# A two-layer encoder on one core: the w_down operands of a seven-product down projection formed beside the up product and kept in DRAM

## The chip, the cores and the metric

The kernel runs on one core of one Trainium2 chip. The metric is the device time of one execution in microseconds (us), the median of the runs. The core has five engines with a queue each: PE (matmul), DVE (VectorE), ACT (ScalarE), POOL (GpSimd) and SP (SyncE), which here issues every transfer. An engine runs its own instructions strictly in their order, and a waiting instruction holds up all those behind it.

## The reference, cut to what matters

Two layers, x of 1024 rows by 1024 columns, all float32. Each layer has four groups of attention heads with an output projection, and then a gated MLP with D_FF = 2816:

```python
h = _rmsnorm(x, norm2_g[l])
u = h @ w_up[l]
...
u = _dwconv3(u, conv_w[l], conv_b[l])
gate, val = split of u into two halves of 2816 columns
x = x + (silu(gate) * val) @ w_down[l]
```

`_dwconv3` is a convolution of width 3 along the rows, one weight per tap and column, and a bias.

## The kernel before, in words

Every product is made in float32 by three matmul passes: an operand is split into a high part (a cast on ACT, L136) and a low part (source minus high part, L132, on DVE or POOL), and PE sums high·high, high·low and low·high. `split` (L128 to L132) does this for all weights.

**The end of the attention** (`tail`). While the last heads finish, PE makes the output projection `od` row block by row block. Each block is added to the residual `xacc`, squared on ACT (L157) for the norm's statistic, scaled to `nx`, transposed by PE (`ntp`, L147) and split into `h2T` (cast L173 on ACT, low part L174 on DVE). `h2T` has two tiles, one for each half of the rows. The order of PE's work here and of the attention is written out by hand in the kernel; the order on the other engines is set by the scheduler that builds the program. `mlp` starts in this stretch: it loads the convolution's weights `cw` (L919, L920) and the first up weights (`load`, L922 to L927).

**The up product** (`mlp`, L913). 44 column blocks of 128 (22 gate blocks, 22 value blocks, taken in pairs). For each, SP loads 512 KB `rawu`, ACT casts it and POOL makes the low part (tile `wu`, three buffers); PE makes 48 matmuls of 128x512 into one of two PSUM buffers `u`; the convolution is one ACT instruction (L939) and two on DVE (L940, L941), which read PSUM. Per pair, ACT makes the Silu (L946) and POOL the product (L948, L952). The first 8 of the 22 gated chunks go to DRAM (`gd`, L949), the other 14 stay in SBUF (`gg`).

**The down product** (`down`, L990). It is a scheme of seven products instead of eight for a 2 by 2 block matrix (table `DOWN`, L978). Each product has 11 steps, each step 12 matmuls of 128x512, so 77 steps and 924 matmuls in each layer. A step has two operands, both made on the spot:

- the gated side: one chunk, or the sum or difference of two chunks (DVE, L1006; 55 of the 77 steps), then cast on ACT and low part on DVE;
- the side of w_down: one or two loads of 256 KB (L1020); where there are two, POOL adds or subtracts them (L1006; 55 steps); then cast on ACT, low part on POOL for odd c and on DVE for even c.

Both lie in one tile `wd` of tag wu, three buffers. Product 0 also reloads the 8 gated chunks from DRAM (`gb`, L1026). At the end of each product DVE adds its sums from PSUM into `xacc` (L1037), 4 or 8 instructions, 48 in each layer.

Of the kernel before, what the change touches and what calls it, by code (L numbers as in the profile page):

```python
# [24 lines left out]
S = 1024  # L25
# [65 lines left out]
class K:  # L91
# [821 lines left out]
    def mlp(self, l, h2T, mp, gd):  # L913
# [8 lines left out]
        def load(jj):  # L922
            raw = self.raw.tile([128, KC, 128], F32, tag="raw", name="rawu")
            nc.sync.dma_start(raw, a["w_up"][l, jj])
            w = mp.tile([128, 2, KC, 128], F32R, tag="wu", name="wu", bufs=3)
            self.split((w[:, 0], w[:, 1]), raw, "act", "pool")
            return w  # L927
# [16 lines left out]
        def gate(j, us):  # L944
# [8 lines left out]
            return t  # L953
# [11 lines left out]
        gp, pm = yield  # L965
        for j in range(1, NFF):
            us = []
            for jj in (j, NFF + j):
                w = load(jj)
                u = pm.tile([128, S], F32, tag="u", name="u", bufs=2)  # L970
                product(u, w, (0, 1))
                us.append(conv(jj, u))
# [17 lines left out]
    def down(self, l, xacc, gs, rx, gp, mp, pm, gd):  # L990

        nc, a = self.nc, self.a
        V, P = nc.vector, nc.gpsimd
        NH = NFF // 2
        todo = [j for c in range(GD // 2) for j in (2 * c, 2 * c + 1)]
        back = {}
        for j in todo[0::2] + todo[1::2]:
            back[j] = gs[j] = gp.tile([128, S], F32, tag=f"b{j}", name="gb")
        order = list(range(GD // 2, NH)) + list(range(GD // 2))

        def operand(w, tag, terms, add, low):
            t = terms[0][0]
            if len(terms) > 1:
                u, sign = terms[1]
                d = mp.tile([128, S], F32, tag="c", name="sum", bufs=3)[:, 0:512] if tag == "ga" else t
                add.tensor_tensor(d, t, u, op=ALU.add if sign > 0 else ALU.subtract)  # L1006
                t = d
            self.split((w[:, 0], w[:, 1]), t, "act", low)
        for n, (As, Bs, Cs) in enumerate(self.DOWN):
# [5 lines left out]
            for i, c in enumerate(order):  # L1015
                raw = (rx if i % 3 == 2 else self.raw).tile([128, 2, 512], F32, tag="raw", name="rawd")
                tb = []
                for q, (k, j, sign) in enumerate(Bs):
                    r0 = (2 * c + k) * 128
                    nc.sync.dma_start(raw[:, q], a["w_down"][l, r0:r0 + 128, j * 512:(j + 1) * 512])  # L1020
                    tb.append((raw[:, q], sign))
                if n == 0 and i >= 1:
                    for _ in range(2):
                        if todo:
                            j = todo.pop(0)
                            nc.sync.dma_start(back[j], gd[j * 128:(j + 1) * 128, :])  # L1026
                w2 = mp.tile([128, 2, 2, 512], F32R, tag="wu", name="wd", bufs=3)
                w, m = w2[:, 0], w2[:, 1]
                operand(w, "ga", [(gs[2 * c + k][:, i * 512:(i + 1) * 512], sign) for i, k, sign in As], V, "dve")
                operand(m, "wd", tb, P, "pool" if c % 2 else "dve")  # L1030
# [112 lines left out]
    def run(self):  # L1143
# [16 lines left out]
        for l in range(self.depth):  # L1160
# [76 lines left out]
            gd = dp.tile([GD * 128, S], F32, tag=f"gd{l}", name=f"gd{l}")  # L1237

# [4 lines left out]
            def mlp():  # L1243
                if "mlp" not in st:
                    ae.close()
                    st["mp"] = me.enter_context(self.pool(f"mp{l}", side=at))
                    h2.append(high.enter_context(self.pool(f"h2b{l}", side=at)).tile([128, 2, KC, 512], F32R, name="h2T1"))
                    st["mlp"] = self.mlp(l, h2, st["mp"], gd)
# [61 lines left out]
            g = st["mlp"].send((ge, pm))  # L1310
            high.close()
            self.down(l, xacc, g, ge, high.enter_context(self.pool(f"Gb{l}", side=at)), st["mp"], pm, gd)
            high.close()
# [35 lines left out]
```

## Time and profile before

| what | us |
|---|---|
| median of three runs | 3204.69 (3200.09 to 3205.86) |
| the profiled execution | 3198.61 |
| its span in the trace | 3196.8 |
| PE busy | 2972.4 (93% of the span) |
| DVE, ACT, POOL busy | 1958.1, 1509.8, 1079.8 |
| mean granted TensorE clock | 0.984 of full |

In the profile's rows a start is given in us from the start of the span; "x12" is the number of instructions that a row joins; what stands in brackets is the idle time of the engine just before, and the instruction that ended it. PEclk is the share of its full clock that TensorE was granted. The first layer's MLP lies at about 845 to 1612 us, the second's at 2433 to 3190 us.

### The profile page before, as it was taken

To read this page: it belongs to the slowest core of one execution; us is meant where nothing else is said; L and a number is where in the kernel's file an instruction comes from. 1 tells how busy PE (TensorE), PEld (TensorE's weight loads), DVE (VectorE), ACT (ScalarE), POOL (GpSimd) and SP (SyncE) were. 2 spreads that over 40 slices of the span, in tenths; PEclk is the share of its full clock that TensorE was granted. 3 is DMA by queue.
4 is the path that set the end of the run, shared out by engine and by line. 5 is a ranking of instruction groups with operands and counts; after the bars stand their busy time and mean duration, and the time that the engine had idled before them with its cause. 6 is when DMAs were issued, how large, how long until landed. Compare 5 with 4: busy or idle time off the path is not lost. (4 is left out here: it accounts for less than half of the span.)

```text
span 3196.8 us, 44677 instructions
## 1 busy us (share of the span) xinstructions
PE 2972.4 (93%) x16536; PEld 2550.3 (80%) x16536; DVE 1958.1 (61%) x3352; ACT 1509.8 (47%) x2873; POOL 1079.8 (34%) x916
## 2 busy tenths in 40 slices
PE   7988899899899999998989899998998999999988
PEld 5978888788788888876779788887886888888767
DVE  6778877777622222277966798777776222223787
ACT  5557765766522222233354677657655222222333
POOL 1265310320133333346522663104102333333464
PEclk9999999999999999999999899999999999999999
DMA  4332241331311111144433322314302211111444
GB/s 144 114 101 67 62 128 39 84 78 45 48 57 69 59 51 49 47 161 158 168 123 111 96 67 70 121 43 93 83 24 41 73 73 54 52 47 69 166 157 161
DMA packets 313162, 275.96 MB, mean 86 GB/s; under 512 B 201200, under 2 KB 246640, under 8 KB 312944
## 3 DMA queue, kind: packets, MB, share of 16 engines
q1 hardware_dynamic: 312944, 273.11, 27.8%
q8 instruction: 130, 2.13, 0.3%
q14 instruction: 88, 0.72, 0.1%
HBM read 212.23 MB, written 50.33 MB: 82 GB/s over the span
## 5 line engine op out<-in xcount | busy, mean ns | idle before, releaser
L143 PE MATMUL u<-h2T,wu 128*128 128x512 f32 x4224 | 963.3, 390 | 0.0
L143 PEld LDWEIGHTS u<-h2T,wu 128*128 128x128 f32 x4224 | 792.7, 188 | 168.9
L940 DVE SCALAR_TENSOR_TENSOR c<-u,cw,c 128x1023 f32<-128x1023 f32 x88 | 112.9, 1282 | 721.2 <-ACT c L939 717.6
L143 PE MATMUL pj<-w,hT 128*128 128x256 f32 (+2 forms) x3072 | 490.0, 313 | 21.3 <-ACT w L136 8.4
L143 PEld LDWEIGHTS pj<-w,hT 128*128 128x128 f32 x3072 | 440.1, 194 | 48.3 <-ACT w L136 9.9
L132 POOL TENSOR_TENSOR wu<-rawu,wu 128x1024 fp32r<-128x1024 f32 x88 | 214.2, 2435 | 626.3 <-ACT wu L136 626.3
L939 ACT ACTIVATE c<-u,cw 128x1024 f32<-128x1024 f32 x88 | 106.2, 1207 | 634.5 <-PE u L143 634.5
L489 ACT CAST PT<-pt 128x512 fp32r<-128x512 f32 x448 | 261.4, 583 | 179.5 <-PE pt L147 170.5
L490 DVE TENSOR_TENSOR PT<-pt,PT 128x512 fp32r<-128x512 f32 x448 | 304.7, 684 | 44.6 <-ACT PT L489 42.1
L147 PE MATMUL pt<-cst,P 128*128 128x128 f32 x1792 | 276.7, 277 | 54.3 <-DVE PT L490 47.9
L143 PE MATMUL d<-wd 128*128 128x512 f32 x1056 | 256.2, 401 | 30.1 <-POOL wd L132 16.7
L143 PEld LDWEIGHTS ot<-PT,v 128*128 128x128 f32 x1664 | 255.4, 192 | 32.0
L147 PEld LDWEIGHTS pt<-cst,P 128*128 128x128 f32 x1792 | 208.1, 142 | 87.8 <-issue 33.8
L143 PE MATMUL ot<-PT,v 128*128 128x256 f32 x1664 | 271.0, 286 | 0.0
L143 PEld LDWEIGHTS d<-wd 128*128 128x128 f32 x1056 | 200.6, 193 | 84.2 <-POOL wd L132 26.1
L143 PE MATMUL S<-k,q 96*128 96x512 f32 (+2 forms) x512 | 209.3, 435 | 17.9 <-DVE nmb L655 16.0
L1006 POOL TENSOR_TENSOR rawd<-rawd 128x512 f32<-128x512 f32 x110 | 164.5, 1496 | 149.5 <-DMA rawd<-in_w_down_dram 145.8
L143 PE MATMUL od<-wo,mT 128*128 128x512 f32 x768 | 202.0, 402 | 0.9 <-DVE mT L1067 0.7
L143 PE MATMUL du<-wd 128*128 128x512 f32 x792 | 186.8, 393 | 12.6 <-POOL wd L132 8.8
L143 PEld LDWEIGHTS du<-wd 128*128 128x128 f32 x792 | 146.9, 188 | 51.6 <-POOL wd L132 13.1
L136 ACT CAST wd<-rawd 128x512 fp32r<-128x512 f32 x154 | 95.4, 619 | 179.6 <-POOL rawd L1006 171.9
L655 DVE CUSTOM_DVE_ANT_0 P<-S,toep 128x1024 f32<-128x1024 f32 x128 | 155.4, 1217 | 25.6 <-PE pt L147 21.7
(212 smaller groups left out, 4565.8 us busy)
## 6 DMA issues: line engine op xcount, KB each, us to landing
rawd<-in_w_down_dram SPq DMA_DIRECT2D x264, 256.0 KB, 3.0
rawu<-in_w_up_dram SPq DMA_DIRECT2D x88, 512.0 KB, 3.2
rawi<-in_w_in_dram SPq DMA_DIRECT2D x20, 512.0 KB, 3.9
rawo<-in_w_out_dram SPq DMA_DIRECT2D x16, 512.0 KB, 3.2
gd<-c SPq DMA_DIRECT2D x16, 512.0 KB, 2.6
gb<-gd SPq DMA_DIRECT2D x16, 512.0 KB, 7.5
sC<-cqk SPq DMA_DIRECT2D x16, 384.0 KB, 2.4
ld<-sB SPq DMA_DIRECT2D x24, 256.0 KB, 3.5
```

Source lines behind the costliest of these rows:

```text
L132: eng.tensor_tensor(dst[1], src, dst[0].bitcast(F32), op=ALU.subtract)
L136: self.nc.scalar.copy(dst, src)
L143: self.nc.tensor.matmul(out, l, r, start=start, stop=stop)
L147: self.nc.tensor.transpose(out, in_, self.ident[:p, :p])
L489: nc.scalar.copy(PT[:, 0, :], pt)
L490: nc.vector.tensor_tensor(PT[:, 1, :], pt, PT[:, 0, :].bitcast(F32), op=ALU.subtract)
L655: nc.vector.tensor_tensor_reduce(out=P, in0=Ps["S", i, s], in1=self.toep[:, o:o + S], scale=-slope, scalar=-NEG, op0=ALU.add, op1=ALU.min, ...
L939: nc.scalar.activation(c, u, AF.Identity, scale=cw[:, 1, jj:jj + 1], bias=cw[:, 3, jj:jj + 1])
L940: nc.vector.scalar_tensor_tensor(c[:, 1:], u[:, :S - 1], cw[:, 0, jj:jj + 1], c[:, 1:], op0=ALU.mult, op1=ALU.add)
L1006: add.tensor_tensor(d, t, u, op=ALU.add if sign > 0 else ALU.subtract)
```

## The change

The side of w_down no longer is formed in `down`. A generator, `prep_down`, does it during the up product: for each of the 77 steps it loads the one or two 256 KB pieces into `rd` (two buffers), adds them on POOL where there are two, splits them on ACT and DVE into `bo` (two buffers) and stores the split pair, 512 KB, to DRAM (`bd`). Two such items stand behind each column block, from pair 1 on. `down` then loads one ready operand of 512 KB for each step; the first two go to `bo`'s buffers, the others to a ring of 8 places in the first tile of h2T, which is dead once the up product has ended. The 8 gated chunks are reloaded into the second tile of h2T; for this the last pair of the up product is made half by half, and the half that reads the second tile comes first. The gated operand gets `wu` for itself, two steps to a buffer, and its low part is made by POOL in every third step (28 of 77) and by DVE in the others. `wu` has two buffers instead of three, and the pool of the MLP's tiles is opened after the second h2T tile instead of before it.

```diff
--- before.py
+++ after.py
@@ -910,7 +910,7 @@
         self.ev(e + 2, self.AV, out)
 
 
-    def mlp(self, l, h2T, mp, gd):
+    def mlp(self, l, h2T, mp, gd, bd):
...
@@ -922,7 +922,7 @@
         def load(jj):
             raw = self.raw.tile([128, KC, 128], F32, tag="raw", name="rawu")
             nc.sync.dma_start(raw, a["w_up"][l, jj])
-            w = mp.tile([128, 2, KC, 128], F32R, tag="wu", name="wu", bufs=3)
+            w = mp.tile([128, 2, KC, 128], F32R, tag="wu", name="wu", bufs=2)
             self.split((w[:, 0], w[:, 1]), raw, "act", "pool")
             return w
 
@@ -950,7 +950,7 @@
                 return None
             t = gp.tile([128, S], F32, tag=f"g{j}", name="gg")
             nc.gpsimd.tensor_tensor(t, v, g, op=ALU.mult)
-            return t
+            return t.rearrange("p (a c) -> p a c", a=2)
 
         ws = [load(jj) for jj in (0, NFF)]
         yield
@@ -963,13 +963,23 @@
             product(u, w, (1,))
         gs = [gate(0, [conv(jj, u) for jj, u in zip((0, NFF), uu)])]
         gp, pm = yield
+        prep = self.prep_down(l, gp, bd)
         for j in range(1, NFF):
-            us = []
+            us, w = [], []
             for jj in (j, NFF + j):
-                w = load(jj)
-                u = pm.tile([128, S], F32, tag="u", name="u", bufs=2)
-                product(u, w, (0, 1))
-                us.append(conv(jj, u))
+                w.append(load(jj))
+                us.append(pm.tile([128, S], F32, tag="u", name="u", bufs=2))
+                if j < NFF - 1:
+                    product(us[-1], w[-1], (0, 1))
+                    us[-1] = conv(jj, us[-1])
+                next(prep, None)
+                next(prep, None)
+            if j == NFF - 1:
+
+                for n in (1, 0):
+                    for i in range(2):
+                        product(us[i], w[i], (n,))
+                us = [conv(jj, u) for jj, u in zip((j, NFF + j), us)]
             gs.append(gate(j, us))
         yield gs
 
@@ -987,47 +997,61 @@
         (((1, 0, 1), (0, 0, -1)), ((0, 0, 1), (0, 1, 1)), ((1, 1, 1),)),
     )
 
-    def down(self, l, xacc, gs, rx, gp, mp, pm, gd):
+    ORDER = tuple(range(GD // 2, NFF // 2)) + tuple(range(GD // 2))
+
+    def prep_down(self, l, gp, bd):
 
         nc, a = self.nc, self.a
-        V, P = nc.vector, nc.gpsimd
+        for n, (_, Bs, _) in enumerate(self.DOWN):
+            for c in self.ORDER:
+                raw = gp.tile([128, 2, 512], F32, tag="rd", name="rawd", bufs=2)
+                for q, (k, j, _) in enumerate(Bs):
+                    r0 = (2 * c + k) * 128
+                    nc.sync.dma_start(raw[:, q], a["w_down"][l, r0:r0 + 128, j * 512:(j + 1) * 512])
+                w = gp.tile([128, 2, 512], F32R, tag="bo", name="wd", bufs=2)
+                if len(Bs) > 1:
+                    nc.gpsimd.tensor_tensor(raw[:, 0], raw[:, 0], raw[:, 1], op=ALU.add if Bs[1][2] > 0 else ALU.subtract)
+                self.split((w[:, 0], w[:, 1]), raw[:, 0], "act", "dve")
+                nc.sync.dma_start(bd[n][c], w.bitcast(F32))
+                yield
+
+    def down(self, l, xacc, gs, gp, h2T, mp, pm, gd, bd):
+
+        nc = self.nc
+        V = nc.vector
         NH = NFF // 2
-        todo = [j for c in range(GD // 2) for j in (2 * c, 2 * c + 1)]
+        todo = list(range(GD))
         back = {}
-        for j in todo[0::2] + todo[1::2]:
-            back[j] = gs[j] = gp.tile([128, S], F32, tag=f"b{j}", name="gb")
-        order = list(range(GD // 2, NH)) + list(range(GD // 2))
...
         for n, (As, Bs, Cs) in enumerate(self.DOWN):
             if n % 2 == 0:
                 ds = [pm.tile([128, 512], F32, tag="d", name="d", bufs=4) for _ in range(4)]
             else:
                 us = [pm.tile([128, S], F32, tag="u", name="du", bufs=2) for _ in range(2)]
                 ds = [u[:, i * 512:(i + 1) * 512] for u in us for i in range(2)]
-            for i, c in enumerate(order):
-                raw = (rx if i % 3 == 2 else self.raw).tile([128, 2, 512], F32, tag="raw", name="rawd")
-                tb = []
-                for q, (k, j, sign) in enumerate(Bs):
-                    r0 = (2 * c + k) * 128
-                    nc.sync.dma_start(raw[:, q], a["w_down"][l, r0:r0 + 128, j * 512:(j + 1) * 512])
-                    tb.append((raw[:, q], sign))
+            for i, c in enumerate(self.ORDER):
+                if n == 0 and i < 2:
+                    m = gp.tile([128, 2, 512], F32R, tag="bo", name="wb", bufs=2)
+                else:
+                    m = h2T[0][:, ring // 4, 2 * (ring % 4):2 * (ring % 4) + 2, :]
+                    ring = (ring + 1) % 8
+                nc.sync.dma_start(m.bitcast(F32), bd[n][c])
                 if n == 0 and i >= 1:
                     for _ in range(2):
                         if todo:
                             j = todo.pop(0)
-                            nc.sync.dma_start(back[j], gd[j * 128:(j + 1) * 128, :])
-                w2 = mp.tile([128, 2, 2, 512], F32R, tag="wu", name="wd", bufs=3)
-                w, m = w2[:, 0], w2[:, 1]
-                operand(w, "ga", [(gs[2 * c + k][:, i * 512:(i + 1) * 512], sign) for i, k, sign in As], V, "dve")
-                operand(m, "wd", tb, P, "pool" if c % 2 else "dve")
+                            nc.sync.dma_start(back[j], gd[j * 128:(j + 1) * 128, :].rearrange("p (a c) -> p a c", a=2))
+                if i % 2 == 0:
+                    w2 = mp.tile([128, 2, 2, 512], F32R, tag="wu", name="ga", bufs=2)
+                w = w2[:, i % 2]
+                t = [gs[2 * c + k][:, q, :] for q, k, _ in As]
+                if len(t) > 1:
+                    d = mp.tile([128, S], F32, tag="c", name="sum", bufs=3)[:, 0:512]
+                    V.tensor_tensor(d, t[0], t[1], op=ALU.add if As[1][2] > 0 else ALU.subtract)
+                    t[0] = d
+                self.split((w[:, 0], w[:, 1]), t[0], "act", "pool" if i % 3 == 1 else "dve")
                 for t in range(4):
                     for p, (x, y) in enumerate(PASSES):
                         self.mm(ds[t], w[:, x, t * 128:(t + 1) * 128], m[:, y, :], i == 0 and p == 0, i == NH - 1 and p == 2)
...
+            bd = [dp.tile([NFF // 2, 128, 2, 512], F32, tag=f"bd{l}_{i}", name=f"bd{l}_{i}") for i in range(7)]
...
             def mlp():
                 if "mlp" not in st:
                     ae.close()
+                    h2.append(high.enter_context(self.pool(f"h2b{l}", side=at)).tile([128, 2, KC, 512], F32R, name="h2T1"))
                     st["mp"] = me.enter_context(self.pool(f"mp{l}", side=at))
-                    h2.append(high.enter_context(self.pool(f"h2b{l}", side=at)).tile([128, 2, KC, 512], F32R, name="h2T1"))
-                    st["mlp"] = self.mlp(l, h2, st["mp"], gd)
+                    st["mlp"] = self.mlp(l, h2, st["mp"], gd, bd)
                 next(st["mlp"])
 
...
@@ -1308,10 +1333,9 @@
             ge = low.enter_context(self.pool(f"G{l}", side=gs))
             pm = me.enter_context(self.pool(f"pm{l}", space=PS))
             g = st["mlp"].send((ge, pm))
+            self.down(l, xacc, g, ge, h2, st["mp"], pm, gd, bd)
+            me.close()
             high.close()
-            self.down(l, xacc, g, ge, high.enter_context(self.pool(f"Gb{l}", side=at)), st["mp"], pm, gd)
-            high.close()
-            me.close()
             low.close()
         for t in range(NT):
             nc.sync.dma_start(self.out[t * 128:(t + 1) * 128, :], xacc[:, t, :])
```

The scheduler orders the engines other than PE anew. Three places where that shows:

ACT at the end of the attention in layer 0, where mT and h2T are the transposed operands of the output projection and of the up product, od the norm's statistic and wu an up weight. Before:

```order
L136 CAST wu<-rawu 128x1024 x2
L1117 CAST mT<-mtp 128x256
L173 CAST h2T_9311<-ntp 128x4x128
L157 ACTIVATE od_9835,nss<-xacc 128x1024
L173 CAST h2T_9311<-ntp 128x4x128
L1117 CAST mT<-mtp 128x256
L136 CAST wu<-rawu 128x1024
L1117 CAST mT<-mtp 128x256
L173 CAST h2T_9311<-ntp 128x4x128
```

The same stretch of ACT now, and behind it the place to which the third cast went:

```order
L136 CAST wu<-rawu 128x1024 x2
L1141 CAST mT<-mtp 128x256
L173 CAST h2T_9318<-ntp 128x4x128
L157 ACTIVATE od_9842,nss<-xacc 128x1024
L173 CAST h2T_9318<-ntp 128x4x128
L1141 CAST mT<-mtp 128x256 x2
L173 CAST h2T_9318<-ntp 128x4x128
...
L173 CAST h2T_9865<-ntp 128x4x128 x4
L136 CAST wd<-rawd 128x512 x2
L939 ACTIVATE c<-u_10063,cw 128x1024
L136 CAST wu<-rawu 128x1024
L136 CAST wd<-rawd 128x512 x2
```

The third cast of an up weight stood between two mT casts and stands behind the last h2T cast and the first convolution now.

SP around the end of the up product in layer 0, where rawd is a piece of w_down, gd and gb the gated chunks in DRAM and in SBUF. Before:

```order
L949 DMA gd_1774<-c 128x1024
L924 DMA rawu<-in_w_up_dram 128x1024 x23
L1020 DMA rawd<-in_w_down_dram 128x512 x8
L1026 DMA gb<-gd_1774 128x1024 x8
L1020 DMA rawd<-in_w_down_dram 128x512 x93
```

Now, from one half of a late pair to the ring's first loads, with bd the split operands in DRAM and rawq, rawk weights of the next layer:

```order
L1010 DMA rawd<-in_w_down_dram 128x512 x2
L1015 DMA bd_6_1781<-wd 128x1024
L1010 DMA rawd<-in_w_down_dram 128x512 x2
L1015 DMA bd_6_1781<-wd 128x1024
L924 DMA rawu<-in_w_up_dram 128x1024
...
L924 DMA rawu<-in_w_up_dram 128x1024 x4
L1223 DMA rawq<-in_c_wqb_dram 128x2x384
L1227 DMA rawk<-in_c_wkvb_dram 128x512
L1045 DMA h2T_9865<-gd_1774 128x1024 x8
L1040 DMA h2T_9318<-bd_0_1775 128x1024 x9
```

The two loads and the store of an item stand by turns with the up loads, and the ring's first loads stand behind the eight reloads.

## Rows read from the trace of the kernel before

**Rows 1.** Timeline of PE, end of the attention, layer 0, then layer 1.

```profile
870.07 1.12 PE L147 MATMUL ntp<-cst,nx 128*128 128x128 f32 x4 [12.17 <-DVE h2T L174]
...
2457.68 1.12 PE L147 MATMUL ntp<-cst,nx 128*128 128x128 f32 x4 [11.58 <-DVE h2T L174]
```

**Rows 2.** Timeline of ACT, the same stretch of layer 0.

```profile
867.48 1.04 ACT L136 CAST wu<-rawu 128x1024 fp32r<-128x1024 f32 x1 [14.59 <-DMA rawu<-in_w_up_dram]
```

**Rows 3.** Timeline of SP (its DMA queue), the same stretch of layer 0.

```profile
848.30 7.81 SPq L919 DMA_DIRECT2D cw<-in_conv_w_dram  x3
...
859.90 11.46 SPq L924 DMA_DIRECT2D rawu<-in_w_up_dram  x3
...
914.11 0.33 SPq L949 DMA_DIRECT2D gd<-c  x1
```

**Rows 4.** Groups of instructions in 1367.6 to 1612 us, the down product, layer 0.

```profile
L143 PE MATMUL d<-wd 128*128 128x512 f32 x528 | 128.3, 400 | 16.8 <-POOL wd L132 10.9 <-ACT wd L136 3.7 <-DVE wd L132 2.2
L143 PE MATMUL du<-wd 128*128 128x512 f32 x396 | 93.5, 393 | 6.7 <-POOL wd L132 4.6 <-DVE wd L132 1.6 <-ACT wd L136 0.5
L1006 POOL TENSOR_TENSOR rawd<-rawd 128x512 f32<-128x512 f32 x50 | 76.6, 1534 | 60.6 <-DMA rawd<-in_w_down_dram 60.4
L136 ACT CAST wd<-rawd 128x512 fp32r<-128x512 f32 x75 | 46.4, 619 | 92.4 <-POOL rawd L1006 89.0 <-DMA rawd<-in_w_down_dram 3.2
L132 DVE TENSOR_TENSOR wd<-rawd,wd 128x512 fp32r<-128x512 f32 x41 | 40.9, 998 | 17.7 <-ACT wd L136 16.5
...
L1037 DVE TENSOR_TENSOR xacc<-xacc,d 128x512 f32<-128x512 f32 x26 | 16.1, 675 | 0.0
```

**Rows 5.** Timeline of PE, the down product, layer 0.

```profile
1367.62 13.81 PE L143 MATMUL d<-wd 128*128 128x512 f32 x60
...
1404.19 6.05 PE L143 MATMUL du<-wd 128*128 128x512 f32 x26
1410.88 24.32 PE L143 MATMUL du<-wd 128*128 128x512 f32 x106 [0.64 <-DVE wd L132]
1435.04 14.82 PE L143 MATMUL d<-wd 128*128 128x512 f32 x64
...
1611.72 1.04 PE L147 MATMUL ntp<-cst,nx 128*128 128x128 f32 x8
1614.86 3.31 PE L143 MATMUL pj<-w,hT 128*128 128x512 f32 x6 [2.10 <-ACT hT L173]
```

**Rows 6.** Timeline of PE, the down product, layer 1: its first and its last row.

```profile
2950.46 13.76 PE L143 MATMUL d<-wd 128*128 128x512 f32 x60
...
3179.64 10.36 PE L143 MATMUL d<-wd 128*128 128x512 f32 x45
```

**Rows 7.** The chain that ended last, the up product of layer 1.

```profile
2477.28 473.36 PE u L143 x2088
```

**Rows 8.** Timeline of all engines, the end of one column block, layer 1.

```profile
2488.26 1.21 ACT L939 ACTIVATE c<-u,cw 128x1024 f32<-128x1024 f32 x1 [10.36 <-PE u L143]
2489.37 1.04 ACT L136 CAST wu<-rawu 128x1024 fp32r<-128x1024 f32 x1
2490.48 2.44 POOL L132 TENSOR_TENSOR wu<-rawu,wu 128x1024 fp32r<-128x1024 f32 x1 [8.12 <-ACT wu L136]
```

**Rows 9.** DMA issues of the page: KB each, median us from issue to landing.

```profile
rawd<-in_w_down_dram SPq DMA_DIRECT2D x264, 256.0 KB, 3.0
...
gd<-c SPq DMA_DIRECT2D x16, 512.0 KB, 2.6
gb<-gd SPq DMA_DIRECT2D x16, 512.0 KB, 7.5
```

**Rows 10.** Stretches: busy us of the engines, granted clock, DMA share, GB/s.

```profile
880.00:1367.00 487.00, 486.04 (x2134) 398.71 (x2135) 121.30 (x99) 122.00 (x120) 160.37 (x71) 1.00 0.15 56
...
1375.00:1385.00 10.00, 6.80 (x31) 5.32 (x30) 5.27 (x7) 2.48 (x4) 3.30 (x3) 1.00 0.95 372
```

**Rows 11.** Tile wd over the whole run: ns min/median/max.

```profile
L132 DVE TENSOR_TENSOR wd<-gg,wd x28: 676/692/2461, 1348.3 to 3030.9; 128x512 fp32r<-128x512 f32 x28
```

More of the change, by code (lines that the diff above doesn't have):

```diff
@@ L988 @@
     )
-    def down(self, l, xacc, gs, rx, gp, mp, pm, gd):
+    ORDER = tuple(range(GD // 2, NFF // 2)) + tuple(range(GD // 2))
+    def prep_down(self, l, gp, bd):
         nc, a = self.nc, self.a
-        V, P = nc.vector, nc.gpsimd
+        for n, (_, Bs, _) in enumerate(self.DOWN):
[13 more added lines that the diff above has]
+        V = nc.vector
         NH = NFF // 2
-        todo = [j for c in range(GD // 2) for j in (2 * c, 2 * c + 1)]
+        todo = list(range(GD))
         back = {}
-        for j in todo[0::2] + todo[1::2]:
-            back[j] = gs[j] = gp.tile([128, S], F32, tag=f"b{j}", name="gb")
-        order = list(range(GD // 2, NH)) + list(range(GD // 2))
[L1001 to L1008, printed above, removed]
+        for i, j in enumerate(todo[1::2] + todo[0::2]):
+            back[j] = gs[j] = h2T[1][:, i // 4, 2 * (i % 4):2 * (i % 4) + 2, :].bitcast(F32)
+        ring = 0
         for n, (As, Bs, Cs) in enumerate(self.DOWN):
```

## The prediction

> **What bounds the kernel now.** The page says PE: 2972.4 of 3196.8 us. Such a share is a mean over stages, so I read the stages that the change touches: first PE's timeline for its gaps, then for each gap the queue of the engine that ends it, then the groups by line.
>
> *End of the attention.* PE stands still for 12.17 us in layer 0 and 11.58 in layer 1, until a low part of h2T comes [rows 1]. ACT, which owes the cast before it, waits 14.59 us for a DMA, inside the third cast of an up weight [rows 2]; its h2T cast is queued behind. The DMA is late because SP spends 7.81 us on the first three loads of the convolution's weights, and begins the three up loads only at 859.90 [rows 3]. PE waits for an operand that it won't need for a long while yet.
>
> *Up product.* PE is busy 486.04 of 487 us at full clock; POOL has 160, DVE 121, ACT 122 of it, and the DMA engines 0.15 [rows 10]. 2088 matmuls take 473.36 us [rows 7], 0.2267 each, so a column block of 48 is 10.88 us. This is the room into which the change puts its work.
>
> *Down product.* It lasts from 1367.62 to 1611.72, 244.1 us, in layer 0 [rows 5], and from 2950.46 to 3190.00, 239.5 us, in layer 1 [rows 6]. PE's waits there sum to 16.8 + 6.7 = 23.5 us, most for POOL's low part of w_down, and POOL waits for loads [rows 4]. Product 1 has one load and no POOL add in a step: 1404.19 to 1435.04, 30.85 us with one wait of 0.64 [rows 5]. It shows what a product costs once the side of w_down is ready.
>
> **The change, part by part.**
>
> 1. *Third up weight.* In the new order ACT's third cast stands behind all h2T casts and the first convolution, with POOL's split behind it. SP still is slow there, but no h2T cast is queued behind the load. Gain 12.17 + 11.58 = 23.8 us. New price: with two wu buffers this weight is made inside the 24 matmuls (5.4 us) that close pair 0, by the convolution 1.21, the cast 1.04 and POOL 2.44 [rows 8], 4.7 us: hidden, with 0.7 to spare. In later blocks the same 4.7 stands against 10.88. The cover gone, up to 1 us a layer; I take 0.
>
> 2. *Down product.* It loses 55 POOL adds, 77 casts and 77 low parts a layer; the gated side stays. All seven products become like product 1: 7 x 30.85 = 216.0. Gain 244.1 - 216.0 = 28.1 and 239.5 - 216.0 = 23.5, together 51.6. What remains on DVE is 55 sums, 49 low parts, about 1.0 us each as the low part of rawd took, and 48 adds of 0.675 [rows 4]: 136 of 216 us. POOL has 28 low parts, no more than 1.5 us each as its adds, 43. ACT has 77 casts of 0.62, 48. Loads: 77 x 0.524 MB in 216 us, 187 GB/s, half of the 372 that a stretch shows [rows 10], and a ring of eight ahead.
>
> 3. *Up product, new work.* Two items in each 10.88 us. The places for `rd` are two, so each place goes round once a block, and its circle must be shorter than a block: low part 1.00, cast 0.62, POOL add 1.53 [rows 4], SP's four issues of 0.33 [rows 3] 1.3, five hand-offs of 0.07 (the 1.04 of a cast that started at 2489.37 to POOL's start at 2490.48 [rows 8]) 0.4, and the landing. The landing is bounded by 2.6 (a store to DRAM alone) and 7.5 (eight reloads at once); the loads of w_down show 3.0 [rows 9]. The stream will be 1.05 MB of stores, 0.90 of loads and 0.52 of up weights in 10.88 us, 227 GB/s, 0.6 of what the DMA engines carry [rows 10], so I take 4.0, near the 3.0 because nothing is issued eight at a time. Sum 8.85, below 10.88. ACT gets 1.2 us a block more, DVE 2.0 and POOL up to 3.1; with what they had [rows 10] that makes POOL 0.6 busy and the other two under 0.45. Cost 0; as PE loses a little wherever a queue is shared, I take 2 us a layer, 4 in all, with 0 and 10 as ends.
>
> 4. *Start of the down product.* The eight reloads (4.19 MB, 11.3 us at 372 GB/s) may start when the last pair's first half is over, 10.9 us before the end, and the ring's first load is queued behind them. The first two steps have their operand already, 24 matmuls or 5.4 us; the third should land some 4 us after the start. I take 1 us a layer, 0 to 3.5 as ends: 2 in all.
>
> 5. *End of a layer.* In layer 0 the first projection waits 2.10 us for a cast on ACT [rows 5]. ACT has fewer casts ahead of it now: -2, with 0 as the other end.
>
> 6. *The rest:* the moved pool, the other order of closing, the last pair by halves (the same 96 matmuls) issue nothing new: 0.
>
> Sum: -23.8 - 51.6 + 4 + 2 - 2 = -71.4 us on the profiled execution's 3198.6: 3127.2. That execution lies 6.1 below the median of the runs, 3204.7, so the median comes to **3133 us**.
>
> **The rivals.**
>
> *A: the preparation paces the up product.* PE doesn't read the prepared operands there, but ACT's and POOL's halves of the next up weight stand in the same queues as their casts and adds, and so wait for w_down's loads. From a landing of 6.0 us on the circle is longer than a block; from 7.0 on it costs 1.0 x 77 blocks of both layers, 77 us, more than the whole gain. At the 7.5 of the reloads it is 12.35, +1.47 x 77 = +113: 3246 us, **slower**. For it: 7.5 has been seen with 0.5 MB transfers, and the stream has four times the rate of before (56 GB/s [rows 10]). Against it: the 7.5 belongs to eight transfers issued together at a DMA share of 0.95.
>
> *B: DVE and POOL hold each other up.* The same low part on DVE took 0.68 us at best and 2.46 at worst [rows 11], and the new work puts POOL's 2.4 us splits beside two DVE low parts in each block. If a low part (0.69 by its median) waits out a whole split of 2.44, and the next add waits out a low part of 0.69, the circle is 8.85 - 1.00 + 0.69 + 2.44 + 0.69 = 11.67, 0.79 over. In half of the 77 blocks that is +30: 3163 us. Against it: the convolutions of the up phase ran beside POOL before, though they read PSUM, and the mean in the down product was 1.00, not 2.46.
> The Trainium skill has a rule for this, "SBUF — State Buffer", section "SBUF: two separate sides": a DVE operation with two SBUF inputs and a GpSimd operation that reads SBUF share a port pair as an exclusive lock, for the whole instruction, whoever starts first. By that rule every meeting costs the rest of the longer one; this trace shows the spread of rows 11 but not a wait of a whole split, so the forecast goes by the mean.
>
> *C: the down product keeps half of its excess,* because DVE's 4 or 8 adds at the end of a product (2.7 to 5.4 us) stand ahead of the gated operands of the next one, and the two `wu` buffers hold only four steps. Half of 51.6 is 26: 3159 us. For it: before, three buffers held three steps of both sides, hardly fewer, and PE waited. Against it: product 1 begins behind the 8 adds of product 0 and waits 0.64 only [rows 5].
>
> *D: the gap at the end of the attention only moves,* since SP's loads still are slow, and PE meets the third weight at once behind pair 0: up to 23.8 back, 3157 us. Against it: between the h2T casts and its third block PE has the 96 matmuls of pair 0, 21.8 us, and the load that ended at 867.48 [rows 2] then is long there.
>
> **How the numbers follow.** Forecast 0.66, C 0.12, D 0.06, B 0.08, A 0.08. The low end: step 3 and 4 at 0 (-6) and seven products without their 0.64 wait (14 x 0.64 = 9): 3133 - 15, about 3117. The high end takes in C, D and B: 3166. Left out: A, and the outermost part of the others, 2 in 10 at most. A measurement of this kernel tells 0.2%, some 6 us, from no change. Faster by more: the forecast, B, C and D, 0.92, less a little for several of them at once, 0.90; within: 0.02; slower: A, 0.08.
>
> **What would show it.** Right: no PE gap over 2 us before the first up block; 2088 matmuls of u within 475 us; d and du from first to last 217 us in each layer, with waits of 1 us at the products' starts. Wrong: PE waiting for POOL's wu within the up product and rawd landing in 6 us or more (A); low parts of over 2 us on DVE there (B); a wait of 2 us at each start of a product, ended by DVE (C); the same 12 us before pair 1, ended by wu (D).

## The result and the profile after

The changed kernel takes 3124.78 us (median of 4 runs, 3121.24 to 3128.84) against 3204.44 before: 79.7 us less, ratio 0.9754 with a 95% interval of 0.9737 to 0.9771. A second time, on another chip, the ratio was 0.9752 (0.9739 to 0.9765). The forecast was 3133, with 3117 to 3166 as its range. The profiled execution has a span of 3120.8 us, 76.0 less than before.

| stage, us | before | after | difference | forecast |
|---|---|---|---|---|
| start to the last `od` block ahead of the gap, layer 0 | 854.9 | 851.6 | -3.3 | 0 |
| from there to the first u, layer 0 | 26.1 | 10.9 | -15.2 | -12.2 |
| up product, layer 0 | 486.6 | 494.5 | **+7.9** | +2 |
| down product, layer 0 | 244.1 | 211.5 | **-32.6** | -27.1 |
| end of layer 0 and attention of layer 1, to the same block | 831.4 | 829.6 | -1.8 | -2 |
| from there to the first u, layer 1 | 25.4 | 10.9 | -14.5 | -11.6 |
| up product, layer 1 | 482.0 | 495.5 | **+13.5** | +2 |
| down product, layer 1 | 239.5 | 209.6 | **-29.9** | -22.5 |

(Each number is a difference of two starts in PE's timeline, the last one a difference to the end of the last matmul; what is behind that is 6.8 us before and 6.7 after.) The sum is near the forecast, but not because each term was: the down product gave 62.5 instead of 49.6, and the up product took 21.4 instead of 4. That two misses of opposite sign nearly cancel is luck.

Rows of the kernel before from which stages of layer 0 begin, and two that are read further down:

```profile
854.88 3.02 PE L143 MATMUL od<-wo,mT 128*128 128x512 f32 x12
872.36 3.88 PE L143 MATMUL od<-wo,mT 128*128 128x512 f32 x12
881.01 5.75 PE L143 MATMUL u<-h2T,wu 128*128 128x512 f32 x24
889.61 478.18 PE L143 MATMUL u<-h2T,wu 128*128 128x512 f32 x2088
```

PE's timeline at the end of the attention in layer 0, after; the gap of [rows 1] is gone:

```profile
851.59 3.02 PE L143 MATMUL od<-wo,mT 128*128 128x512 f32 x12
854.45 1.04 PE L147 MATMUL ntp<-cst,nx 128*128 128x128 f32 x8
855.24 3.00 PE L143 MATMUL od<-wo,mT 128*128 128x512 f32 x12
...
862.49 5.75 PE L143 MATMUL u<-h2T,wu 128*128 128x512 f32 x24
```

ACT's timeline, then SP's. The third cast of an up weight now follows the first convolution directly and has lost the 14.59 us of [rows 2]; SP still needs 7.99 us for three loads, and PE doesn't wait for what they delay:

```profile
882.35 1.21 ACT L939 ACTIVATE c<-u,cw 128x1024 f32<-128x1024 f32 x1 [6.20 <-PE u L143]
883.45 1.04 ACT L136 CAST wu<-rawu 128x1024 fp32r<-128x1024 f32 x1
...
844.95 7.99 SPq L919 DMA_DIRECT2D cw<-in_conv_w_dram  x3
```

PE's timeline of the down product, layer 0. No row has a wait; [rows 5] had them in most:

```profile
1357.01 5.66 PE L143 MATMUL d<-wb,ga 128*128 128x512 f32 x24
1362.51 24.88 PE L143 MATMUL d<-h2T,ga 128*128 128x512 f32 x108
1387.23 30.38 PE L143 MATMUL du<-h2T,ga 128*128 128x512 f32 x132
1417.44 30.38 PE L143 MATMUL d<-h2T,ga 128*128 128x512 f32 x132
...
1568.51 1.03 PE L147 MATMUL ntp<-cst,nx 128*128 128x128 f32 x8
```

From one product's start to the next it is 30.21 us, 132 matmuls of 228.9 ns. In layer 1 it is 29.92, 226.7 ns:

```profile
2904.51 5.60 PE L143 MATMUL d<-wb,ga 128*128 128x512 f32 x24
...
3084.03 30.08 PE L143 MATMUL d<-h2T,ga 128*128 128x512 f32 x132
```

The up product, layer 0: a group by line in 870 to 1357 us, then PE's timeline, then a DMA issue of the page:

```profile
L132 DVE TENSOR_TENSOR wd<-rawd,wd 128x512 fp32r<-128x512 f32 x77 | 116.9, 1522 | 128.8 <-ACT wd L136 128.6
```

```profile
912.45 444.73 PE L143 MATMUL u<-h2T,wu 128*128 128x512 f32 x1920 [2.52 <-DVE c L941]
```

```profile
rawd<-in_w_down_dram SPq DMA_DIRECT2D x264, 256.0 KB, 5.1
```

A low part of the preparation takes 1.52 us and a piece of w_down 5.1 to land, where the forecast had 1.00 and 4.0 (the landing of [rows 9] was 3.0). Apart from 0.97 us at its start, as before, PE waits once, 2.52 us for the convolution. ACT's timeline shows why: the convolution's first instruction stands behind a cast of the preparation, which waited 8.16 us for its piece of w_down:

```profile
907.94 0.62 ACT L136 CAST wd<-rawd 128x512 fp32r<-128x512 f32 x1 [8.16 <-POOL rawd L1013]
908.47 1.20 ACT L939 ACTIVATE c<-u,cw 128x1024 f32<-128x1024 f32 x1
```

But the 1920 matmuls of the one row take 444.56 us to the next row's start, 231.5 ns each. Before, 2088 matmuls of this layer took 478.01 us (889.61 to 1367.62), 228.9 ns each, and those of layer 1 took 226.7 [rows 7]. So most of what the up product lost stands in no wait: the matmuls follow each other more slowly, at full granted clock but for 4 us behind the wait (last section). The time from one matmul's start to the next is called the pace here. The experiments begin there.

### The profile page after: what moved, and what is told of

The parts are those of the page before. It is cut to its first block, busy times and chain, and to the rows that moved or that the text cites. A ratio compares the mean times of both kernels' runs of the same rounds, so it can differ in the third digit from the quotient of the medians.

```text
span 3120.8 us, 45434 instructions
## 1 busy us (share of the span) xinstructions
PE 2965.2 (95%) x16536; PEld 2551.4 (82%) x16536; DVE 2017.8 (65%) x3366; ACT 1508.5 (48%) x2873; POOL 1049.8 (34%) x902
## 5 line engine op out<-in xcount | busy, mean ns | idle before, releaser
L143 PE MATMUL u<-h2T,wu 128*128 128x512 f32 x4224 | 979.4, 393 | 5.3 <-DVE c L941 5.2
L143 PEld LDWEIGHTS pj<-w,hT 128*128 128x128 f32 x3072 | 438.5, 194 | 47.2 <-ACT w L136 10.8
L132 DVE TENSOR_TENSOR wd<-rawd,wd 128x512 fp32r<-128x512 f32 x154 | 233.0, 1518 | 233.7 <-ACT wd L136 233.2
L143 PE MATMUL d<-h2T,ga 128*128 128x512 f32 x1008 | 230.9, 390 | 0.0
L143 PEld LDWEIGHTS d<-h2T,ga 128*128 128x128 f32 x1008 | 189.3, 188 | 40.3
L143 PE MATMUL du<-h2T,ga 128*128 128x512 f32 x792 | 181.4, 390 | 0.0
L143 PEld LDWEIGHTS du<-h2T,ga 128*128 128x128 f32 x792 | 148.7, 188 | 31.7
```

Source lines behind the costliest of these rows:

```text
L132: eng.tensor_tensor(dst[1], src, dst[0].bitcast(F32), op=ALU.subtract)
L143: self.nc.tensor.matmul(out, l, r, start=start, stop=stop)
```

## The experiments

### Is the slower pace the preparation's doing, or the place of the tiles?

The forecast had no term for it. Two things changed in the up product: the preparation runs beside it, and `wu` and the second h2T tile, one of the two moving tiles (the operands of 512 columns), lie elsewhere. **First**, the preparation was left out:

```diff
-                next(prep, None)
-                next(prep, None)
+                if j == NFF // 2:
+                    next(prep, None)
...
-                nc.sync.dma_start(m.bitcast(F32), bd[n][c])
+                nc.sync.dma_start(m.bitcast(F32), bd[0][self.ORDER[i % 2]])
```

> The changed kernel, but only two of the 77 items of each layer are prepared, and every load of the down product reads one of these two (so the output is not the reference's: the side of w_down is wrong in all but two steps). All tiles stay where they are. In the changed kernel the up product takes 494.5 and 495.5 us against 486.6 and 482.0 before, 21.4 more; its matmuls follow each other every 230.9 and 231.7 ns, against 228.9 and 226.7 before. Theory P (place): the slower pace comes from where the tiles lie and not from the preparation; then the pace stays 230 to 232 here, the up product loses only its waits of 2.5 to 4 us a layer, and the time is 3116 to 3119. Rival C (contention by the preparation's transfers or engine work): the pace is back at 228.9 and 226.7, the up product at 486 and 482, and the time at 3103. Down product 211.5 and 209.5 by both.

PE's timeline, layer 0 and layer 1:

```profile
879.32 481.84 PE L143 MATMUL u<-h2T,wu 128*128 128x512 f32 x2088
1361.00 3.37 PE L143 MATMUL d<-wb,ga 128*128 128x512 f32 x14
...
2430.00 481.91 PE L143 MATMUL u<-h2T,wu 128*128 128x512 f32 x2088
2911.74 3.56 PE L143 MATMUL d<-wb,ga 128*128 128x512 f32 x15
```

481.7 us for 2088 matmuls, 230.7 ns, in both layers, with no wait and next to no preparation. The pace isn't contention with the preparation. (The time, one run, was 3129.94, not the 3116 to 3119 expected: the stretches ahead of the first u of layer 0 and between the two MLPs each took some 8.3 us longer than in the changed kernel's profile; in the first the mean granted clock was 0.97 instead of 0.98. Totals of single executions can't show a few us here; stages can.)

**Second**, only the transfers of the preparation, without its adds, casts and low parts:

```diff
-                for q, (k, j, _) in enumerate(Bs):
+                for q, (k, j, _) in enumerate(Bs if len(Bs) > 1 else Bs * 2):
...
-                w = gp.tile([128, 2, 512], F32R, tag="bo", name="wd", bufs=2)
...
-                nc.sync.dma_start(bd[n][c], w.bitcast(F32))
+                nc.sync.dma_start(bd[n][c], raw)
```

> The changed kernel with the preparation's loads and stores but without its adds, casts and low parts (raw pieces are stored, and where there is one piece it is loaded twice; the output is not the reference's). Theory P (place): pace of the up matmuls 230 to 232 ns as in the changed kernel, no PE waits for the convolution at the start, time 3116 to 3119. Rival C1 (transfers disturb PE): the same slow pace, which goes away when no item is prepared. Rival C2 (DVE, POOL and ACT work disturbs PE): pace back at 228.9 and 226.7 ns, time 3103. Landing of the pieces of w_down: by the theory that DMA load sets it about 5 us as in the changed kernel (5.1), by the rival that waiting engines set it 3 us.

3179.63 us, slower than the changed kernel, although it does less. The pace is 230.8 and 230.7 ns, as theory P says. But PE waits 18.1 us in layer 0 (groups by line, 860 to 1387 us):

```profile
L143 PE MATMUL u<-h2T,wu 128*128 128x512 f32 x2112 | 496.9, 396 | 18.1 <-POOL wu L132 12.6 <-ACT wu L136 5.5
```

Of the 57 us between the two profiled executions 42 lie in the up products. Here a place of `rd` is held until its store has landed (4.0 us for the load, 3.6 for the store), and the next up load stands on SP behind stores and loads that wait for one another. That nobody had expected. It is rival A's kind of wait, through SP's queue instead of ACT's and POOL's: PE never reads these tiles, and still waits for them.

**Third**, the pools in the order of before, which moves tiles and changes nothing else (every engine has the same instructions in the same order):

```diff
-                    h2.append(high.enter_context(self.pool(f"h2b{l}", side=at)).tile([128, 2, KC, 512], F32R, name="h2T1"))
                     st["mp"] = me.enter_context(self.pool(f"mp{l}", side=at))
+                    h2.append(high.enter_context(self.pool(f"h2b{l}", side=at)).tile([128, 2, KC, 512], F32R, name="h2T1"))
...
-            me.close()
             high.close()
+            me.close()
```

> The changed kernel with the two pools opened and closed in the order of the kernel before, so that wu, the convolution's tiles and the second h2T tile lie elsewhere; nothing else differs. Theory P (place): the pace of the up matmuls changes, towards 228.9 and 226.7 ns, and the time falls by up to 15 us, to 3110. Rival C (contention by the preparation): pace 230.9 and 231.7 ns and a time within 5 us of 3125.

One run, 3122.32 us; pace 229.4 and 226.8 ns. It was timed again (sixth run), and then beside the changed kernel on one chip (ninth and tenth):

> The same kernel as in the third experiment (the changed kernel with the pools in the order of before), timed. Theory: the pace of the up matmuls is again 229.4 and 226.8 ns, and about half of the 12 us that this is worth is lost again to waits in the up product, since a block of 10.88 us is hardly longer than the preparation's circle: 2 to 7 us faster than the changed kernel, ratio to the kernel before 0.973 to 0.975. Rival (the placement's gain is whole): 0.9715. Rival (no gain): 0.9754.

> The changed kernel as it is, timed beside the next two on one chip. Theory: pace of the up matmuls 230.7 and 231 ns as in its first profile, since the tiles lie where they lay; ratio to the kernel before 0.975.

> The changed kernel with the pools in the order of before, beside the changed kernel on one chip. Theory (place): pace 229 and 226.8 ns again, ratio 0.972 to 0.973, some 5 to 9 us faster than the ninth. Rival: equal within 2 us.

Sixth: 3117.43 us, 0.9722 (0.9701 to 0.9743). Ninth, the changed kernel: 3126.34, 0.9752 (0.9739 to 0.9765). Tenth, the same with the pools as before: **3117.82 us, 0.9724 (0.9711 to 0.9737)**. The two intervals don't touch, so the place of tiles is worth some 8.5 us by these medians (6.3 us in the up products of the two profiled executions), and this version beats both kernels. PE's timeline in layer 1, first of the ninth, then of the tenth:

```profile
2498.64 410.02 PE L143 MATMUL u<-h2T,wu 128*128 128x512 f32 x1776 [1.00 <-DVE c L941]
2908.50 3.79 PE L143 MATMUL d<-wb,ga 128*128 128x512 f32 x16
```

```profile
2497.32 197.00 PE L143 MATMUL u<-h2T,wu 128*128 128x512 f32 x868 [1.08 <-DVE c L941]
2694.77 11.17 PE L143 MATMUL u<-h2T,wu 128*128 128x512 f32 x48 [0.45 <-POOL wu L132]
2706.50 10.29 PE L143 MATMUL u<-h2T,wu 128*128 128x512 f32 x44 [0.56 <-POOL wu L132]
2717.44 185.24 PE L143 MATMUL u<-h2T,wu 128*128 128x512 f32 x816 [0.65 <-DVE c L941]
2902.52 2.65 PE L143 MATMUL d<-wb,ga 128*128 128x512 f32 x11
```

409.86 us for 1776 is 230.8 ns; 185.08 for 816 is 226.8. With the faster pace PE's waits in the two up products grow from 5.4 to 9.4 us, for POOL's wu too: a block of 10.88 us leaves the preparation hardly any room.

**What about a place matters** was asked of the last run. In the built programs the address of a moving tile within its partition, modulo 128, was 32 wherever the pace was 228.9, and 96 wherever it was 226.7; blocks whose matmuls go by turns through one tile of each kind had the 230.7 and more. In the tenth kernel both tiles of layer 0 have 32; the edit moves each by 64 bytes:

```diff
...
+                    if l == 0:
+                        self.nc.vector.memset(hb.tile([128, 16], F32, name="pad1"), 0.0)
...
+                    if l == 0:
+                        self.nc.vector.memset(ha.tile([128, 16], F32, name="pad0"), 0.0)
...
```

> As the tenth, with 64 bytes of padding beside each of the two h2T tiles of layer 0, so that their addresses within a partition go from 32 to 96 above a multiple of 128 (59424 and 167200 to 59488 and 167136). In the traces so far a matmul whose moving operand begins at 96 above has a pace of 226.7 ns, one at 32 above 228.9, and by turns of the two 230.7 to 231.7; wu always lies at 96 above. Theory A (this offset sets the pace): in layer 0 the up product and the down product go from 228.9 to 226.7 ns, as in layer 1; 2112 and 924 matmuls by 2.2 ns make 4.6 and 2.0 us, of which the up product may lose 1 to 3 to longer waits for the preparation; 4 to 6 us faster than the tenth, ratio 0.9705 to 0.971. Rival B (the layer or the side of the memory sets it, the offset is chance): pace 228.9 in layer 0, ratio 0.9724.

3126.26 us, 0.9749 (0.9736 to 0.9762): 8 us slower than the tenth, which ran on another chip, and neither theory's number. Only 4.1 us of it are located, in the down product of layer 0. PE's timeline of layer 0's down product:

```profile
1387.83 30.96 PE L143 MATMUL du<-h2T,ga 128*128 128x512 f32 x132
1418.63 30.96 PE L143 MATMUL d<-h2T,ga 128*128 128x512 f32 x132
```

30.80 us for 132 matmuls, 233.3 ns, where the changed kernel had 228.9: the first h2T tile, moved by 64 bytes, got a new and worse pace. The starts of single matmuls show that those which read the second tile alone (the end of pair 0) went to 226.7, as theory A says. So the place does it, in steps as small as 64 bytes, and the offset modulo 128 is not the rule. Modulo 256 the same addresses differ: 59424 and 167200 both leave 32, and became 59488 and 167136, which leave 96 and 224. In the built programs of the kernel before, the changed one, the tenth and this one all ten places of an h2T tile fit this: 224 with 226.7 ns, 32 with 228.9, and 96, which occurs once, with 233.3. No run was made to test this and no other remainder occurs, so the rule stays open.

### How near was the preparation to pacing the up product?

> The changed kernel with one rd buffer instead of two, so that both items of a column block go through the same place, one after the other. Theory: the preparation's circle (load, add, cast, low part, the next load's issue) is about 10.5 us and not the 8.85 of the forecast, since a piece of w_down lands in 5.1 us and a low part takes 1.52; with one place a block of PE lasts two circles, so the up product grows by 8 to 11 us in 38 blocks of each layer, 300 to 420 us, and the time is 3750 to 3900; PE waits there for POOL's wu and for the convolution. By the forecast's 8.85 it would be 6.8 us a block, 260 us a layer, 3640. Rival (PE does not depend on the preparation through the queues): the time stays under 3200 and the preparation is only late for the down product.

(The edit is `bufs=1` instead of `bufs=2` for `rd`.) 3377.16 us, far under all that was expected of the theory. PE's timeline at the start of the down product in layer 0:

```profile
1479.09 5.46 PE L143 MATMUL d<-wb,ga 128*128 128x512 f32 x12 [72.03 <-DMA wb<-bd]
```

The blocks are not tied to two items each: the up product takes 544.9 us instead of 494.5, and then the down product waits 72.03 us for operands that aren't ready. The rival is half right. From the first load's issue at 867.3 to the end of the last low part at 1479.5 the 77 items take 7.95 us each. With this run's own landing (3.9) and low part (0.69 at the median) the forecast's sum gives 8.4 for an item of two pieces, 6.6 for one of the 22 without an add and a second load, 7.9 in the mean. Its terms were right, then; two of its sizes were not, under the load of two places: 8.85 + 1.1 (landing) + 0.5 (low part) = 10.5, an estimate, against blocks of 10.9 to 11.1. So the margin was about 0.5 us, not 2.0. In the changed kernel's trace no margin shows in the products with two pieces: by the ends of the low parts in layer 0 two items took 10.8 to 12.3 us there, and 8.5 and 9.3 in the two products with one piece (how much of that the circle set and how much the order of the queues, isn't separated). All 77 took 10.66 us for two, and were done 79 us ahead of the down product.

Two attempts to shorten that circle, both with the pools as before. One transfer for two neighbouring pieces, and then also a later begin:

```diff
...
+                    nc.sync.dma_start(raw, a["w_down"][l, r0:r0 + 256, j * 512:(j + 1) * 512].rearrange("(q p) c -> p q c", p=128))
...
+                    nc.sync.dma_start(raw, a["w_down"][l, r0:r0 + 128, :].rearrange("p (q c) -> p q c", q=2))
...
```

> As the sixth, and the two pieces of an item come in one transfer of 512 KB where they are neighbours in DRAM (44 of the 55 items that have two). Theory (the circle is at its limit, and SP's issues and the second landing are in it): the circle gets shorter by 0.5 to 1 us, PE's waits in the up product fall from 3.3 and 6.2 us to under 2 in each layer, and the time falls by 3 to 7 us against the sixth. Rival (the waits come from the landing under load, whatever the number of transfers): no change.

```diff
-                next(prep, None)
-                next(prep, None)
+                if j > 1:
+                    next(prep, None)
+                    next(prep, None)
...
```

> As the seventh, and the preparation begins with pair 2 instead of pair 1. Theory (the wait of 2.7 us for the convolution early in the up product comes from the first items, whose casts stand ahead of the convolution in ACT's queue while the loads are late): that wait goes, 2 to 6 us faster than the seventh over both layers. Rival: the first items are as late whenever they begin, and the same wait appears one pair later: no change. Against it: the last items come in the last pair, and the down product's start could wait for them by some us.

Seventh: 3131.59 us, 0.9767 (0.9742 to 0.9793); eighth: 3129.5, 0.9761 (0.9735 to 0.9787). Both are worse than the sixth, 3117.43, on the same chip. DMA issues of the seventh's page:

```profile
rawd<-in_w_down_dram SPq DMA_DIRECT2D x88, 512.0 KB, 6.1
rawd<-in_w_down_dram SPq DMA_DIRECT2D x88, 256.0 KB, 5.3
```

The one large transfer lands in 6.1 us, later than the small ones of this run in 5.3 and of the sixth in 5.1, and low parts have a median of 2.21 us instead of 1.49. PE's waits in the two up products grow from 8.3 us in the sixth to 12.7. So fewer issues didn't shorten the circle. Of the 15.3 us between the two profiled executions 6.3 lie in the up products; most of the rest lies in the attention, which the edit doesn't touch, and stays open.

The eighth run says nothing about a later begin, because there was none: the scheduler put the preparation back. Its first loads are issued 5.17 us behind the first u, as in the seventh. The first u and SP's first loads of w_down, seventh, then eighth:

```profile
864.01 5.75 PE L143 MATMUL u<-h2T,wu 128*128 128x512 f32 x24
869.18 0.89 SPq L1012 DMA_DIRECT2D rawd<-in_w_down_dram  x2
...
864.67 5.75 PE L143 MATMUL u<-h2T,wu 128*128 128x512 f32 x24
869.84 0.89 SPq L1013 DMA_DIRECT2D rawd<-in_w_down_dram  x2
```

Whether the first items would be late whenever they begin is therefore open.

The adds on DVE instead of POOL:

```diff
-                    nc.gpsimd.tensor_tensor(raw[:, 0], raw[:, 0], raw[:, 1], op=ALU.add if Bs[1][2] > 0 else ALU.subtract)
+                    nc.vector.tensor_tensor(raw[:, 0], raw[:, 0], raw[:, 1], op=ALU.add if Bs[1][2] > 0 else ALU.subtract)
```

> As the tenth, and the preparation's 55 adds of a layer are made by DVE instead of POOL. Theory (the preparation's circle is at the length of a block because DVE's low parts and POOL's instructions hold each other up, 1.52 us a low part beside 0.69 at best, and because the adds stand behind POOL's splits): POOL's work in the up product falls from 237 to about 160 us a layer, the mean low part to 1.0 to 1.2 us, PE's waits in the up product from 3.4 and 4.9 us to under 2, and the time by 3 to 6 us against the tenth. Rival L (the waits come from the landing of 5.1 us alone): the low parts get shorter but the waits stay. Rival D (DVE with 55 more instructions is later with the convolution): the waits for DVE's convolution grow, 2 to 8 us slower than the tenth.

3145.66 us, 0.9807 (0.9793 to 0.9822), 28 us slower than the tenth. Tile wd (ns min/median/max), then PE's timeline in layer 0:

```profile
L132 DVE TENSOR_TENSOR wd<-rawd,wd x154: 672/684/2901, 878.8 to 2845.6; 128x512 fp32r<-128x512 f32 x154
```

```profile
922.63 145.63 PE L143 MATMUL u<-h2T,wu 128*128 128x512 f32 x624 [8.01 <-DVE c L941]
```

The median low part falls from 1.48 us in the tenth to 0.68: DVE and POOL did hold each other up. Rival D has the direction, though the loss is far over its 2 to 8 us: a DVE add that waits for a landing stands ahead of the convolution that frees PE's buffer. DVE's timeline just ahead of the wait:

```profile
917.30 2.68 DVE L1013 TENSOR_TENSOR rawd<-rawd 128x512 f32<-128x512 f32 x1 [1.60 <-DMA rawd<-in_w_down_dram]
919.90 1.27 DVE L940 SCALAR_TENSOR_TENSOR c<-u,cw,c 128x1023 f32<-128x1023 f32 x1
```

PE waits 13.6 and 14.0 us a layer for the convolution, 8.01 at once, and the two up products take 27.0 us more than in the tenth. The low part got shorter, but two items still took 11.03 us in layer 0 (10.63 in the tenth), and the wait moved to a queue where it costs more.

### Where the gap at the end of the attention came from

The kernel **before**, with the convolution's weights laid out as the tile wants them:

```diff
-        for i in range(3):
-            nc.sync.dma_start(cw[:, i, :], a["conv_w"][l, i].rearrange("(j p) -> p j", p=128))
-        nc.sync.dma_start(cw[:, 3, :], a["conv_b"][l].rearrange("(j p) -> p j", p=128))
+        nc.sync.dma_start(cw[:, 0:3, :], a["conv_w"][l])
+        nc.sync.dma_start(cw[:, 3, :], a["conv_b"][l])
...
+        elif n == "conv_w":
+            v = v.reshape(DEPTH, 3, 2 * NFF, 128).transpose(0, 3, 1, 2)
+        elif n == "conv_b":
+            v = v.reshape(DEPTH, 2 * NFF, 128).transpose(0, 2, 1)
```

> The kernel before with the convolution's weights laid out beforehand as the tile wants them, so that SP spends about 1 us on them instead of 11.5; the order of ACT stays, the third cast of an up weight still between two mT casts. Theory: the gap at the end of the attention came from SP's late third up load, through ACT's queue; it shrinks from 12.2 and 11.6 us to 2 us or less, and the time falls by 20 to 30 us, to 3175 to 3185. Rival (the third cast waits for its raw buffer or its wu buffer, not for SP): the gap stays over 8 us and the time over 3195.

3179.63 us against 3212.96 for the kernel before on the same chip, one run each, 33 less. ACT's, SP's and PE's timelines:

```profile
855.40 1.05 ACT L136 CAST wu<-rawu 128x1024 fp32r<-128x1024 f32 x1 [1.46 <-DMA rawu<-in_w_up_dram]
...
849.35 0.41 SPq L918 DMA_DIRECT2D cw<-in_conv_w_dram  x1
849.82 0.42 SPq L919 DMA_DIRECT2D cw<-in_conv_b_dram  x1
...
864.18 1.09 PE L147 MATMUL ntp<-cst,nx 128*128 128x128 f32 x8 [1.26 <-POOL nx L165]
```

The third cast stands where it stood and waits 1.46 us instead of 14.59; PE's longest wait there is 1.26 in layer 0. So the chain SP, late load, ACT's queue, h2T is shown from its other end. The change cut it at ACT's queue; it could have been cut at SP. About 26 of the change's 80 us could be had by this small edit alone: from the same `od` block to the first u it is 12.7 us in layer 0 (855.93 to 868.66) and 12.8 in layer 1 (2436.68 to 2449.44), 13.4 and 12.6 less than before.

## Why the prediction was right, and where it wasn't

**Step 1, the third up weight: right, a little small.** It counted the gap alone, 23.8. The two stretches gave 29.7, since behind the gap twelve matmuls took 3.88 us before, at a granted clock of 0.71, and take 3.00 now, and small waits went too.

**Step 2, the down product: right in its mechanism, mis-sized.** "All seven products become like product 1: 7 x 30.85" kept that product's wait of 0.64 seven times, which was itself a wait for an operand. Measured: 30.21 and 29.92 us, the difference being the two paces, which no term had (before, product 1 took 30.85 and 30.90). 13 us better than the forecast with its transition; 9 of it was named as the low end.

**Step 3, the up product: the step that failed,** though the sum and the direction came out. "Cost 0; ... I take 2 us a layer, 4 in all, with 0 and 10 as ends" measured 21.4, outside its ends. Some 14 of that is the pace (230.7 instead of 228.9, and 231.4 instead of 226.7 ns, by 2112 matmuls), 5.2 are PE's waits for the convolution, and most of the rest is a stretch at 0.57 of the clock after the first of them. The sum over queues was sound in that PE waits little, but by less than it said: the circle was 10.5 us by the estimate above, not 8.85. Its own sign of being right, 2088 matmuls of u within 475 us, failed: with their waits they took 485.9 in layer 0 and 486.9 in layer 1. And the sentence that closed the list, "*The rest:* the moved pool ... 0", put at nothing what makes about half of the excess: the ninth and tenth runs show that this edit cost some 8.5 us, and the first that the pace stays without the preparation.

**Step 4, the start of the down product: right,** even the 2 us weren't lost. **Step 5** took 2 and found 1.8, together with all of the attention, whose own noise is as large.

**Rival A** did not come, but it was near: landing 5.1 where 6.0 decides. Its mechanism is real (second and fifth runs, and the 2.52 us of the changed kernel itself). **Rival B** was true of DVE: low parts went from a mean of 1.00 to 1.52 us with a maximum of 2.89, and from a median of 1.48 to 0.68 without POOL's adds. What it cost PE by itself no run shows. By the Trainium skill ("SBUF — State Buffer", "SBUF: two separate sides") a DVE operation with two SBUF inputs and a GpSimd operation that reads SBUF exclude each other for the whole of the instruction that started first (not, as the prediction puts it, for the rest of the longer one). The trace agrees: the longest low part, 2.89, is the shortest, 0.68, and nearly a whole POOL split of 2.4. **C and D** did not come: no product begins with a wait, and pair 1 begins without one.

## What to carry to other kernels

Work put beside the engine that sets the time is not free just because the other engines have room. Write down the circle of the scarce buffer, with the landing and the instruction times that hold under the new load, and compare it with the period it must fit. An engine that never reads the new tiles still waits for them if its own operands stand behind them in a queue; a wait for a transfer belongs in the queue that releases least. And after any change, divide a long row without waits by its count: a pace that changed is in no list of waits.

## What the runs showed of the hardware that was not expected

- The pace of 128x512 float32 matmuls at full granted clock depends on where the moving tile lies: 226.7, 228.9 or 233.3 ns from one tile, 230 to 231.4 by turns from two that differ. It was the same within 0.7 ns in every execution of the same placement, and did not change when the work beside it was left out (230.7). A shift of 64 bytes took one tile from 228.9 to 233.3 and another from 228.9 to 226.7. Which property of the address does it, is open. The Trainium skill's list of who holds up whom ("SBUF — State Buffer", "Who interferes with whom") has PE sharing its SBUF ports with no other engine; the first run agrees, since the pace stayed at 230.7 ns without the work beside it.
- In the seventh run a transfer of 512 KB of w_down landed in 6.1 us, one of 256 KB in 5.3 (medians).
- PE's wait of 2.52 us that ended at 912.45 was followed by a stretch of lower clock, 0.57 granted from 912 to 916; from 916 on it shows 1.00, and behind the waits of 1.41 and 1.27 us in layer 1 it stayed at 1.00. Columns as in [rows 10]:

```profile
912.00:916.00 4.00, 3.55 (x9) 2.89 (x10) 1.60 (x2) 1.06 (x1) 2.29 (x2) 0.57 0.72 237
916.00:930.00 14.00, 14.00 (x62) 11.35 (x62) 7.76 (x6) 4.57 (x7) 7.81 (x5) 1.00 0.76 275
```
